# A two-layer hybrid decoder step: operand reloads by quarters, an earlier reload, and the second layer's modulation moved

## The chip, the cores and the metric

The kernel runs on one core of one Trainium2 chip. The metric is the device time of one execution in microseconds (us); the kernel before has a median of 2805.24 us over 3 runs (2802.8 to 2806.19). One further execution was taken by the profiler; all rows below come from it.

## The reference

One inference step of a two-layer trunk on 1024 prompt tokens and 8 sample tokens, in float32. Every layer has a token mixer and an MLP; both get a normalised input that is scaled and shifted by a modulation computed from a condition `c`, and both are gated by it:

```
for l in range(DEPTH):                              # 2 layers, D_MODEL = 1024
    mod = silu(c) @ ada_w[l] + ada_b[l]             # 6 * 1024 columns a layer
    sh1, s1, g1, sh2, s2, g2 = split(mod, 6)
    h = rmsnorm(x, norm_mix[l]) * (1 + s1) + sh1
    out = even_mixer(h) if l == 0 else mamba_mixer(h)
    x = x + g1 * out
    h = rmsnorm(x, norm_mlp[l]) * (1 + s2) + sh2
    x = x + g2 * (square(relu(h @ mlp_w1[l])) @ mlp_w2[l])
y = rmsnorm(x, norm_final)
```

The even mixer is a gated linear recurrence beside a short gated convolution, with one input and one output projection; the odd one is a state-space mixer. The recurrent states are returned too.

## The kernel before, in words

**Stages.** The program is one stream of work in four stages, each with its own pools of tiles: the even mixer, the first MLP, the odd mixer, the second MLP. Activations are kept transposed, features on the 128 partitions and the 1032 tokens along a row. Every float32 product of a GEMM is made of three matmuls: weights and activations are each split into a rounded part and a remainder (`hi`, `lo`), and `mm3` (L486) issues hi*hi, hi*lo and lo*hi into one PSUM sum (its three matmuls are L490, L493 and L494). ScalarE (ACT) makes `hi` by a copy, VectorE (DVE) `lo` by a subtraction: L466/L467 and others in `prep` for weights, L843/L844 for the MLP's second operand.

**Work order.** `work_order` lists every weight unit (128 x 1024) in the order of its use. `need` (L478) hands out the next one and calls `prepare`, which keeps the units ahead loaded and split: loads go from SP's queue (`dma`, L221), with two buffers for raw weights and three for split ones. `need` also calls `ada_steps(ada_rate[0])`, so that the modulation's generator makes one step a unit. `Background.tick` (L147) advances other generators (norms, recurrences) between tiles. Other transfers go from POOL's queue through `dma_aux` (L227). Some instructions are pinned to program order (`keep_in_program_order`); otherwise the framework places them in its queues, and each queue runs in order.

**Modulation.** `ada_gen` (L288) works for groups of four blocks of 512 modulation columns. A step loads four tiles of 256 KB (`t<-ada`), `depth` steps ahead, and adds one 128-row slice of the four blocks at once in PSUM (L320). After a group's eight steps a tail copies the sum, transposes it (L332) and adds the bias (L344). One layer's weights are 25 MB. In the even stage the rest of layer 0's modulation (blocks 6 to 11) runs during the last projections, one step a `need` (L1327), in tiles taken by turns from two pools (`t2` with 8, `t3` with 14 buffers). All of layer 1's runs in the first MLP's second half, one step a unit from unit 8 on (L942, L1927), in tiles from `t2` and `t6` (4 double buffers, which the weights of some products use as well).

**The MLP** is written as two levels of seven block products (a Strassen-like scheme) instead of eight. Its first half makes 16 pairs of hidden blocks, seven products each (`AOPS`). The last four pairs (12 to 15) make their products 1 and 2 first (`FRONT`): results are spilled to DRAM (`keep`, `B`) and come back later (`kept`, L854, `t<-kept`; the B12 block, `x<-b`). Product 6 of pair 12 subtracts from the reloaded tile at L899; it is the next one after `FRONT`. The seven operands of the second half are stored to DRAM while the hidden blocks are made (`td<-x`).

The second half (L938 on) does seven products of eight units each (`BOPS`, product index `i` from 0, unit `j` in 0 to 7), the last one in two halves by tokens. A unit takes a quarter `q` of the operand: units 0 to 3 use quarters 0 to 3 for the first two output blocks, 4 to 7 use them again for the other two; product 0 has its own order. `load_op` (L833) brings one half of an operand (two quarters) back in four DMAs of 516 KB into two tiles, one for `hi`, one for `lo`; three pairs of such tiles are used in rotation (`BSET`), so a half is asked for when the half three before it is done: after unit 5 of the product before, or after unit 7 of the one before that (L977). `split_op` issues the splits of loaded parts, so many after each unit as the tables at L974 to L976 say. In products 2 and 3 of this count each unit of weights is a sum of two loaded blocks and is also stored (`sd<-t`).

Of the kernel before, what the change touches and what calls it, by code (L numbers as in the profile page):

```python
# [14 lines left out]
P = 128  # L15
D = 1024
KT = 8
# [114 lines left out]
class Background:  # L132


    def __init__(self):
        self.gens = []
        self.width, self.rate, self.due = 2, 1.0, 0.0

# [23 lines left out]
def kernel(ctx: ExitStack, tc: tile.TileContext, A: dict):  # L162
# [188 lines left out]

    ada, ada_rate = [iter(())], [1]

# [431 lines left out]
    def mlp(l, gi, finish, more=None):  # L785
# [47 lines left out]
        def load_op(i, kh):  # L833

            pool, tag = ((big, M["tags"][0]), (ph.pool, "hr"), (big, M["tags"][1]))[BSET[i][kh]]
            ts = [pool.tile([P, KT * 520], F32R, name="rr", tag=tag, bufs=2) for _ in range(2)]
            hi, lo = R[i, kh] = [t[:, 0:KT * HX].rearrange("p (k t) -> p k t", t=HX) for t in ts]
            d = td[BOPND[BPROD[i]]][kh]

            def parts():  # L840
                for c in range(0, KT, 2):
# [4 lines left out]
            for c in range(0, KT, 2):  # L846
# [18 lines left out]
        for i, (p, q) in enumerate(AOPS):  # L865
# [55 lines left out]
            if (p, q) == FRONT[1][-1]:  # L921
                load_op(0, 0)
            elif p == NPAIR - 2 and q in (7, 5, 4, 3):
                split_op()
            if (p, q) == (NPAIR - 1, 5):
                split_op(4)
                load_op(0, 1)
# [5 lines left out]
        load_op(1, 0)  # L933
        acc = tp.tile([P, KT, NS], F32, name="racc", tag="racc", bufs=2)
# [4 lines left out]
        for n, (i, hb, q, mp) in enumerate(BOPS):  # L939
            j = n % 8  # L940
            hi, lo = need(f"b{l}", n, AHEAD - 1)
            if n == 8 and more:  # L942
# [3 lines left out]
            rh, rl = R[i, q // 2]  # L946
            seq = BSEQ if i else BFIRST
            qs = [qq for qq, mm in seq if mm == mp]
            for m in (2 * mp, 2 * mp + 1):
# [3 lines left out]
                for b in range(2) if hb is None else (hb,):  # L953
                    c = slice(b * hw, b * hw + hw)
                    mm3(pt[:, b, 0:hw], [(hi[:, o:o + P], lo[:, o:o + P], rh[:, k, c], rl[:, k, c])
                                         for k, o in ((q % 2 * 4 + k, 256 * k + m % 2 * P) for k in range(4))],
# [1171 lines left out]
```

## Time and profile before

| What | Value |
|---|---|
| median of 3 runs | 2805.24 us |
| the profiled execution | 2806.7 us |
| its span, first to last instruction | 2804.9 us |
| PE busy in 300 to 500 us (even layer's end) | 200 of 200 us |
| longest idle of PE in the first MLP's first half's last pairs | 5.29 us at 835.37 |
| the same in the second MLP | 6.56 us at 2396.69 |
| first MLP's second half, product 0 to 5 | 883.5 to 1223.3 us |
| second MLP's second half, product 0 to 5 | 2444.2 to 2736.1 us |
| HBM read and written | 408.59 MB, 113.80 MB |

Rows of waits read: who waited <- for whom: us in total, times, longest. Rows of the timeline: start, length, engine, line, operation, tiles written <- read, count, and in brackets the idle time before and what ended it. An instruction's row names a line of the kernel; `L490` to `L494` are the three matmuls of all GEMMs. The granted clock is the share of full speed that TensorE's throttle allowed.

### The profile page before, as it was taken

The page shows a single profiled execution, that of the slowest core. Times are in us where ns is not written, and L with a number is a line of the kernel's source. Part 1 is how long each engine was busy: PE and PEld are TensorE (multiplying, and loading weights), DVE is VectorE, ACT ScalarE, POOL GpSimd, SP SyncE. Part 2 cuts the span into 40 slices and gives each one's busy share as a digit, 9 for nine tenths or more (in the row PEclk, how much of TensorE's full clock was granted, in tenths as well). Part 3 has the DMA queues.
Part 4 walks back from the last instruction along what each step waited for, and adds up shares of the span by engine and source line. Part 5 has one row for each costly group of instructions (what it writes and reads, how often), then busy time and mean ns, then how long its engine had stood idle before and what let it go on. Part 6 is the DMA issues. An engine that isn't in the chain of part 4 may idle for free. (4 is left out here: it accounts for less than half of the span.)

```text
span 2804.9 us, 49250 instructions
## 1 busy us (share of the span) xinstructions
PE 2654.7 (95%) x19442; PEld 2443.9 (87%) x19442; DVE 1983.5 (71%) x3668; ACT 1485.0 (53%) x2409; POOL 266.5 (10%) x492
## 2 busy tenths in 40 slices
PE   6999999999999988998899999999999999999897
PEld 4889888899999977898789897787779999999897
DVE  5666544788757555775789788998778776756676
ACT  5785511464444322356687767878756445433234
POOL 0000000023223100000000000000001322311000
PEclk9999999999999999999899999999999999999998
DMA  8232333257468899834545745444435655779764
GB/s 300 69 107 71 105 121 113 88 191 242 168 204 312 328 334 353 321 129 115 142 148 144 184 122 155 132 132 124 117 105 172 223 184 181 264 284 372 266 214 156
DMA packets 199256, 525.63 MB, mean 187 GB/s; under 512 B 32688, under 2 KB 50736, under 8 KB 199024
## 3 DMA queue, kind: packets, MB, share of 16 engines
q1 hardware_dynamic: 150640, 355.25, 40.3%
q0 software_dynamic: 48384, 167.23, 16.2%
q8 instruction: 153, 2.51, 0.4%
q14 instruction: 79, 0.65, 0.1%
HBM read 408.59 MB, written 113.80 MB: 186 GB/s over the span
## 5 line engine op out<-in xcount | busy, mean ns | idle before, releaser
L490 PE MATMUL pg<-hh,whi 128*128 128x256 f32 (+2 forms) x1616 | 535.8, 332 | 13.5 <-ACT hh L592 6.2
L493 PE MATMUL pd<-rr,whi 128*128 128x258 f32 x1792 | 512.3, 286 | 25.1 <-DVE rr L844 24.9
L493 PE MATMUL pg<-hl,whi 128*128 128x256 f32 (+2 forms) x1616 | 522.8, 324 | 1.9 <-DVE hl L593 1.9
L494 PE MATMUL pg<-hh,wlo 128*128 128x256 f32 (+2 forms) x1616 | 522.0, 323 | 0.0
L490 PE MATMUL pd<-rr,whi 128*128 128x258 f32 x1792 | 513.4, 287 | 0.0
L494 PE MATMUL pd<-rr,wlo 128*128 128x258 f32 x1792 | 510.5, 285 | 1.5 <-DVE wlo L467 1.1
L467 DVE TENSOR_TENSOR wlo<-raw,whi 128x1024 fp32r<-128x1024 f32 x222 | 270.7, 1221 | 216.5 <-ACT whi L466 209.9
L466 ACT CAST whi<-raw 128x1024 fp32r<-128x1024 f32 x222 | 231.4, 1044 | 349.4 <-PE pg L493 192.0
L493 PEld LDWEIGHTS pd<-rr,whi 128*128 128x128 f32 x1792 | 343.6, 192 | 29.2 <-DVE rr L844 27.0
L490 PEld LDWEIGHTS pd<-rr,whi 128*128 128x128 f32 x1792 | 343.7, 192 | 19.0 <-issue 16.5
L490 PEld LDWEIGHTS pg<-hh,whi 128*128 128x128 f32 x1616 | 308.0, 191 | 50.0 <-issue 8.8
L494 PEld LDWEIGHTS pd<-rr,wlo 128*128 128x128 f32 x1792 | 344.0, 192 | 4.0 <-DVE wlo L467 1.8
L493 PEld LDWEIGHTS pg<-hl,whi 128*128 128x128 f32 x1616 | 308.1, 191 | 31.1 <-issue 5.8
L494 PEld LDWEIGHTS pg<-hh,wlo 128*128 128x128 f32 x1616 | 307.4, 190 | 24.4 <-issue 0.7
L490 PE MATMUL pd<-hh,whi 128*128 128x258 f32 x1024 | 293.9, 287 | 18.6 <-DVE t L899 12.6
L493 PE MATMUL pd<-hh,whi 128*128 128x258 f32 x1024 | 292.7, 286 | 0.8 <-DVE hh L695 0.8
L494 PE MATMUL pd<-hh,wlo 128*128 128x258 f32 x1024 | 291.1, 284 | 0.0
L490 PEld LDWEIGHTS pd<-hh,whi 128*128 128x128 f32 x1024 | 196.8, 192 | 21.0 <-issue 13.6
L456 ACT CAST whi<-t 128x1024 fp32r<-128x1024 f32 x64 | 67.0, 1047 | 274.8 <-PE pd L493 116.8
L493 PEld LDWEIGHTS pd<-hh,whi 128*128 128x128 f32 x1024 | 196.3, 192 | 1.9 <-DVE hh L695 1.4
L494 PEld LDWEIGHTS pd<-hh,wlo 128*128 128x128 f32 x1024 | 196.6, 192 | 0.0
L490 PE MATMUL pg<-ffh,whi 128*128 128x264 f32 (+2 forms) x544 | 176.8, 325 | 2.1 <-ACT bcz L1633 1.5
(335 smaller groups left out, 5813.9 us busy)
## 6 DMA issues: line engine op xcount, KB each, us to landing
raw<-W SPq DMA_DIRECT2D x375, 512.0 KB, 4.3
td<-x POOLq DMA_DIRECT2D x224, 258.0 KB, 3.6
rr<-td POOLq DMA_DIRECT2D x112, 516.0 KB, 8.1
t<-ada SPq DMA_DIRECT2D x192, 256.0 KB, 5.4
t<-W SPq DMA_DIRECT2D x32, 512.0 KB, 5.8
sd<-t SPq DMA_DIRECT2D x32, 512.0 KB, 5.8
t<-sd SPq DMA_DIRECT2D x32, 512.0 KB, 5.5
t<-csd SPq DMA_DIRECT2D x64, 256.0 KB, 4.6
```

The source lines that it names most:

```text
L456: S.copy(hi, h)
L466: S.copy(hi, raw)
L467: V.tensor_sub(lo, raw, hi.bitcast(F32))
L490: mm = PE.matmul(pt, wh, xh, start=first and i == 0, stop=False)
L493: PE.matmul(pt, wh, xl, start=False, stop=False)
L494: PE.matmul(pt, wl, xh, start=False, stop=last and i == n - 1)
```

## The change

It does three things.

- **Operand loads by quarters.** `load_op(i, q)` loads one quarter, `hi` and `lo` side by side in one tile, in two DMAs of the same 516 KB. A tile is free when its quarter's last unit is done. From product 1 on, quarters 2 and 3 of the next product are asked for after units 4 and 5, quarters 0 and 1 of the one after that after units 6 and 7 (product 0: after 2, 3, 6, 7). The split tables follow.
- **One reload earlier.** The tiles that pairs 12 and 13 need from DRAM, and pair 12's B12 block, are asked for at product 1 of pair 15, two products earlier than before, and so ahead of the four loads of the second half's first operand instead of behind them.
- **Two thirds of layer 1's modulation** (blocks 0 to 7, 16 steps and two tails) run in the even layer's end after layer 0's rest, loaded two steps ahead. Steps there are no longer tied to `need`: `mm3` counts its columns, and `Background.tick` makes a step whenever 8200 more have gone by. Blocks 8 to 11 (8 steps, one tail) stay in the first MLP's second half, one step in four units from unit 4 on. `ada_rate` is 0 from there on.

```diff
     def tick(self, n=1):
 
+        if self.between:
+            self.between()
...
+    cols, ada_cols = [0, 0], 8200
+
+    def ada_between():
+        while cols[0] >= cols[1]:
+            cols[1] += ada_cols
+            ada_steps(1)
...
     def mm3(pt, trip, first=True, last=True):
         n = len(trip)
+        cols[0] += 3 * n * trip[0][2].shape[-1]
...
-        def load_op(i, kh):
-
-            pool, tag = ((big, M["tags"][0]), (ph.pool, "hr"), (big, M["tags"][1]))[BSET[i][kh]]
-            ts = [pool.tile([P, KT * 520], F32R, name="rr", tag=tag, bufs=2) for _ in range(2)]
-            hi, lo = R[i, kh] = [t[:, 0:KT * HX].rearrange("p (k t) -> p k t", t=HX) for t in ts]
-            d = td[BOPND[BPROD[i]]][kh]
+        def load_op(i, q):
+
+            pool, tag = ((big, M["tags"][0]), (ph.pool, "hr"), (big, M["tags"][1]))[BSET[i][q // 2]]
+            t = pool.tile([P, KT * 520], F32R, name="rr", tag=tag, bufs=2)
+            hi, lo = R[i, q] = [t[:, j * 4 * HX:(j + 1) * 4 * HX].rearrange("p (k t) -> p k t", t=HX)
+                                for j in range(2)]
+            d = td[BOPND[BPROD[i]]][q // 2][:, q % 2 * 4:q % 2 * 4 + 4]
...
-            if p in SPLIT and q == (5 if p < 2 else 6):
+            if p in SPLIT and q == (5 if p < 2 else 6) and p != NPAIR - TAIL:
                 dma_aux(slot(p, 1), B[p])
+            elif (p, q) == (NPAIR - 1, 1):
+                kept(NPAIR - TAIL)
+                kept(NPAIR - TAIL + 1)
+                dma_aux(slot(NPAIR - TAIL, 1), B[NPAIR - TAIL])
...
-            if n == 8 and more:
+            if n == 0 and more:
                 ada[0] = more()
             elif i == 6 and hb == 0 and j == 0:
                 ada_steps(99)
+            elif n % 4 == 0:
+                ada_steps(1)
...
-            if i == 0:
-                split_op((0, 2, 2, 0, 1, 1, 2, 0)[j])
-            else:
-                split_op((2, 2, 1, 1, 1, 1, 0, 1)[j] if i == 1 else (2, 1, 1, 1, 1, 1, 0, 1)[j] if i < 6 else (2, 1, 0, 0, 0, 0, 0, 0)[j] if hb == 0 else 0)
-            if j == (5 if i else 3) and i < 6:
-                load_op(i + 1, 1)
-            elif j == 7 and i < 5:
-                load_op(i + 2, 0)
+            split_op(((0, 2, 1, 1, 1, 1, 1, 1), (2, 2, 1, 1, 1, 1, 0, 2), (1, 1, 0, 0, 0, 0, 0, 0))[2 if i == 6 else i][j]
+                     if i in (0, 1, 6) else (1, 1, 1, 1, 1, 1, 0, 2)[j])
+            at = (4, 5, 6, 7) if i else (2, 3, 6, 7)
+            if j in at and i < 6 and i + 1 + at.index(j) // 2 < 7:
+                load_op(i + 1 + at.index(j) // 2, (2, 3, 0, 1)[at.index(j)])
...
-        ada[0] = ada_gen(0, alloc, ((6, 7, 8, 9), (10, 11)))
+
+        def gens():
+            yield from ada_gen(0, alloc, ((6, 7, 8, 9), (10, 11)), 2)
+            yield from ada_gen(1, alloc, ((0, 1, 2, 3), (4, 5, 6, 7)), 2)
+        ada[0], ada_rate[0] = gens(), 0
+        cols[1], bg.between = cols[0], ada_between
...
         bg.width = 1
+        bg.between = None
...
-        mlp(0, mi(0, 5), to_odd, more=lambda: ada_gen(1, alloc, ((0, 1, 2, 3), (4, 5, 6, 7), (8, 9, 10, 11))))
+        mlp(0, mi(0, 5), to_odd, more=lambda: ada_gen(1, alloc, ((8, 9, 10, 11),)))
```

More of the change, by code (lines that the diff above doesn't have):

```diff
@@ L845, in parts @@
                     yield
-            for c in range(0, KT, 2):
+            for c in range(0, 4, 2):
                 dma_aux(lo[:, c:c + 2].bitcast(F32), d[:, c:c + 2])
@@ L926, in mlp @@
                 split_op(4)
-                load_op(0, 1)
+                load_op(0, 2)
+                load_op(0, 3)
             bg.tick(2)
@@ L955, in mlp @@
                     mm3(pt[:, b, 0:hw], [(hi[:, o:o + P], lo[:, o:o + P], rh[:, k, c], rl[:, k, c])
-                                         for k, o in ((q % 2 * 4 + k, 256 * k + m % 2 * P) for k in range(4))],
+                                         for k, o in ((k, 256 * k + m % 2 * P) for k in range(4))],
                         q == qs[0], q == qs[-1])
```

7 lines of the change are left out of this document (5 added, 2 removed).

## The prediction

> **What bounds the kernel now.** I read the page's head first, then TensorE (PE) in windows cut at the products' first matmuls, then who PE waited for in the windows that fall short, then the queues behind those waits.
>
> ```profile
> span 2804.9 us, 49250 instructions
> ...
> PE 2654.7 (95%) x19442; PEld 2443.9 (87%) x19442; DVE 1983.5 (71%) x3668; ACT 1485.0 (53%) x2409; POOL 266.5 (10%) x492
> ```
>
> PE is busy for 95% of the span, so the change can only pay where PE stands still or runs at half clock, and whatever it adds to a full PE costs its whole length. The windows below give PE, PEld, DVE, ACT and POOL (us busy, instructions), then the granted clock, the DMA share and GB/s.
>
> ```profile
> 650.00:700.00 50.00, 50.00 (x420) 50.00 (x419) 41.05 (x69) 21.35 (x36) 16.51 (x31) 1.00 0.70 237
> 810.00:850.00 40.00, 34.71 (x272) 34.54 (x271) 21.24 (x35) 15.03 (x27) 11.27 (x21) 0.91 0.63 211
> 2370.00:2410.00 40.00, 33.44 (x267) 33.26 (x267) 20.89 (x35) 14.67 (x26) 11.29 (x21) 0.91 0.60 207
> 1000.50:1010.80 10.30, 5.49 (x25) 5.49 (x26) 8.62 (x10) 2.00 (x2) 0.00 (x0) 0.50 0.94 350
> 883.50:929.50 46.00, 46.00 (x387) 46.00 (x386) 22.50 (x26) 18.91 (x21) 14.35 (x27) 1.00 1.01 388
> 929.50:983.70 54.20, 54.20 (x443) 47.37 (x441) 31.99 (x42) 17.03 (x18) 4.98 (x10) 1.00 0.86 303
> 983.70:1119.20 135.50, 116.72 (x885) 101.64 (x882) 72.68 (x99) 31.07 (x33) 7.57 (x15) 0.91 0.95 342
> 1119.20:1170.30 51.10, 51.10 (x422) 47.21 (x421) 38.27 (x47) 18.85 (x20) 4.18 (x8) 1.00 0.91 335
> 1170.30:1223.30 53.00, 47.97 (x386) 47.76 (x385) 32.06 (x39) 19.00 (x21) 4.19 (x8) 0.94 0.51 190
> 2490.20:2536.20 46.00, 46.00 (x387) 46.00 (x386) 29.90 (x40) 16.06 (x16) 4.19 (x8) 1.00 0.61 210
> 2536.20:2640.00 103.80, 94.37 (x770) 93.75 (x770) 71.84 (x92) 32.08 (x32) 8.37 (x16) 0.97 0.89 332
> 2640.00:2689.50 49.50, 46.48 (x386) 46.07 (x386) 36.99 (x46) 16.99 (x18) 4.19 (x8) 1.00 0.74 257
> 2689.50:2736.10 46.60, 46.34 (x386) 46.03 (x385) 31.99 (x39) 18.90 (x21) 4.19 (x8) 1.00 0.54 193
> 362.90:511.80 148.90, 148.90 (x957) 124.72 (x960) 66.28 (x134) 24.96 (x39) 0.00 (x0) 1.00 0.32 102
> ```
>
> The first row is the MLP's full rate: 420 matmuls in 50 us, 8.4 a us, 0.119 us each. A product of the MLP's second half is 8 units of 48 matmuls: 46.0 us, as 883.5 to 929.5 shows (product 0 of the first MLP; 1 to 5 follow, the windows 983.7 and 2536.2 holding products 2 and 3). The first MLP's products 1 to 5 take 54.2 + 135.5 + 51.1 + 53.0 = 293.8 us against 5 x 46.0 = 230.0; the second MLP's, without modulation, 46.0 + 103.8 + 49.5 + 46.6 = 245.9. The waits of PE in 800 to 850, 950 to 1250 and 2500 to 2750, and one matmul of the second MLP's first half, say why.
>
> ```profile
> PE pd L490 <- DVE t L899: 5.3, 1, 5.3
> ...
> PE pd L493 <- DVE rr L844: 12.4, 2, 7.4
> PE pd L320 <- DMA t<-ada: 11.2, 3, 4.9
> ...
> PE pd L493 <- DVE rr L844: 12.4, 5, 7.1
> ...
> 2396.69 0.55 PE L490 MATMUL pd<-hh,whi 128*128 128x258 f32 x1 [6.56 <-DVE t L899]
> ```
>
> Three places, then: a reloaded tile late for L899 (both MLPs), split operands late (both), modulation weights late (first MLP). Each is a transfer.
>
> **The change part by part.** *The early reload.* POOL's queue around the first stall:
>
> ```profile
> 816.61 0.54 POOL L227 DMA_DIRECT2D kept<-t  x1 [0.70 <-ACT t L893]
> 823.01 0.54 POOL L227 DMA_DIRECT2D b<-t  x1 [5.86 <-ACT t L804]
> 823.54 2.12 POOL L227 DMA_DIRECT2D rr<-td  x4
> 825.65 1.08 POOL L227 DMA_DIRECT2D t<-kept  x2
> ```
>
> The reload (t<-kept) that L899 needs is issued behind four operand loads of 516 KB. The change issues it two products (5.7 us) before those, near 816.6, where POOL is idle. The stall was 5.3 us with the reload at 825.65, so 9 us earlier leaves nothing to wait for; late next is only the weight preparation, whose windows before show no wait. Nothing waits behind the moved issues but the stores at 816.61 and 823.01, by at most 1.6 us, and their readers come much later. Saved: at 8.4 a us the windows 810 and 2370 should hold 336 and hold 272 and 267, so 64 and 69 are missing, 7.6 + 8.2 = 15.8 us. I leave 0.8 as residue: **-15.0** (bounds -16 and -11, should DVE's queue give 5 back).
>
> *Operand loads by quarters.* Today half an operand, 2.1 MB, is asked for at once, twice within 11.5 us:
>
> ```profile
> 2573.32 2.09 POOL L227 DMA_DIRECT2D rr<-td  x4 [34.73 <-PE pd L494]
> 2584.81 2.09 POOL L227 DMA_DIRECT2D rr<-td  x4 [9.40 <-PE pd L494]
> ```
>
> In products 2 and 3 each unit also moves 1.57 MB of weights and stored sums. From the first burst to the first use of that half, four units (23 us), 4.2 + 6.3 = 10.5 MB are wanted: 456 GB/s, over the 388 that the fullest window shows. Weights land late, DVE blocks on them, and the split behind them in its queue (L844) is late. With quarters of 1.06 MB after units 4, 5, 6 and 7, the same 4.2 MB share six units (34.5 us) with 9.4 MB: 395 GB/s, about what the queues carry, and the needed quarter is split one unit earlier. Products 4 and 5 store nothing and want less. The number of DMAs and of L843/L844 instructions stays the same. New is that a split issued one unit after its load can hold ACT and DVE; behind it stand the weight preparations, due two units (11.5 us) later, which covers one landing of the median here:
>
> ```profile
> rr<-td POOLq DMA_DIRECT2D x112, 516.0 KB, 8.1
> t<-ada SPq DMA_DIRECT2D x192, 256.0 KB, 5.4
> ```
>
> The second MLP loses 245.9 - 230.0 = 15.9 us today; I expect 3 to stay: **-12.9** (bounds -16 and 0).
>
> *Two thirds of the modulation moved.* The groups of L320 in the even layer's window and in the first MLP's second half, and three waits of the queues (SP's in the two stretches, DVE's in the second):
>
> ```profile
> L320 PE MATMUL psm<-t,ct x88: 592/592/617, 362.9 to 511.4; 128*32 128x512 f32 x88
> ...
> L320 PE MATMUL pd<-t,ct x192: 592/617/1061, 941.1 to 1141.4; 128*32 128x512 f32 x192
> ...
> SPq L221 <- PE psm L320: 50.0, 5, 21.0
> ...
> SPq L221 <- DMA sd<-t: 52.7, 14, 9.8
> ...
> DVE t L455 <- DMA raw<-W: 26.4, 7, 8.6
> ```
>
> 192 matmuls are 24 steps of 8. Product 1 took 54.2 - 46.0 = 8.2 us more with 7 of them: 1.17 us each. So of the first MLP's 293.8 - 230.0 = 63.8 us, 24 x 1.17 = 28.1 are modulation, about 1.4 (an estimate from the same row: ten matmuls' worth) its three transposing tails, and 34.3 are stalls. 16 steps and two tails move: 16 x 1.17 + 0.9 = 19.6 us leave here and arrive in the even layer, where the window 362.9 to 511.8 has PE busy for all of its 148.9 us. That is **0**: no idle time there to fill.
>
> What moves for profit is 16 x 1.05 = 16.8 MB of reads, from windows with a DMA share of 0.86 to 0.95 to one with 0.32 and 102 GB/s. What stays in the first MLP is one step in four units. Products 2 and 3 then want the second MLP's 332 x 103.8 = 34.5 MB and four steps, 38.7 MB. PE needs 92.0 + 4 x 1.17 = 96.7 us for them. At 342 GB/s that is 113 us, at 388 100 us, and at 332/0.89 = 373 104 us: 3 to 16 us too long, less what three prepared units (about 4 MB, 10 us) carry over. I take 6 there, nearest to 373, and 3 for the other products, where product 0 is full already (share 1.01) and gets one step more; one of four double tiles is held by a waiting step throughout, which the 52.7 us that SP waited for stores to free such tiles warns of. Of 34.3 us 9 stay: **-25.3** (bounds -34 and -11). The Trainium skill's page "HBM Reference", section "Specifications (TRN2)", puts a core streaming alone at about 425 GB/s; by that figure the 38.7 MB take 91 us, PE is the bound and the sum comes out 6 us lower. The trace disagrees while it is full: 342 at a share of 0.95.
>
> In the even layer a step is due every 8200 columns: 8200/258 x 0.119 = 3.8 us of matmuls and 1.1 of its own, 4.9 us. The tiles are loaded two steps ahead: 8.7 us, against four issues and a landing of 5.4, some 7 us. Where two steps fall on one tick (a 512-token block is 12,288 columns) the lead shrinks. SP's queue is in order, and the tiles come from two pools. A walk through the ticks with a landing of 4.5 us gives 2 us of waits, with 6 us 8. I take **+3** (bounds 0 and +10).
>
> *Sum.* -15.0 - 12.9 + 0 - 25.3 + 3 = -50.2. The profiled execution took 2806.7 us (span 2804.9): 2756.5. It stood 1.5 above the median of the runs, 2805.24, so against that: **2755**.
>
> How much a stall costs beyond its idle time matters here. The idle times are 5.3 + 6.6, 23.6 and 12.4, 47.9 us, and I count 15.8 + 34.3 + 15.9 = 66.0, since PE comes back at half clock: in the row 1000.5 to 1010.8 the clock is 0.50 throughout, over 5.5 us of restarted work. The Trainium skill, "TensorE: Matmul & The Clock Gate", Part 1, says that work is slow for about one window of 3.4 us after an idle window; by that rule six stalls over 3.4 us add 1.7 each, 58.1 in all, and the change would end 8 us later, near 2763. The 5.5 us of this trace stand against it.
>
> **The rivals.** *Transfers stay the bound.* The bytes are the same but for the moved reads, and their shape in time matters little. Then products 2 and 3 of the first MLP take 113 us, 16 too many, its product 5 keeps its 7 us (53.0 against 46.0), so 23 of 34.3 stay; the second MLP keeps its 15.9. Gain 11.3 + 15.0 - 3 = 23.3: 2782. For it speaks the share of 1.01 in product 0; against it the 0.61 in the second MLP's product 1, idle just before the bursts. The Trainium skill, "DMA: Bandwidth & Descriptors", section "Issuing engines are not separate DMA queues", would side with it, as transfers of all queues share 16 engines; no product's window here beats 388, however many queues run.
>
> *Modulation starves the even layer.* If pools or SP's order leave only one step in flight, a load asked for at one step meets the next 3.8 us later, needs 7, and PE waits 3.2 us in each of 28 steps: 90 us, which makes 2755 - 3 + 90 = 2842, slower. It decides from a lead of one step on; at half the steps it would cost 45 and end near 2797. For it speak the 50.0 us that SP waited for L320 to free tiles, up to 21.0 at once, with one step in flight; against it 8 and 14 tiles in the two pools, of which the convolutions hold some 8, leaving three steps' worth.
>
> *The change does little of what it says.* Where pins are off, instructions are placed by the framework, and reload and quarters could end up behind the same loads; with no gain in transfers either: 2800 to 2810.
>
> **How the numbers follow.** The forecast has 0.75, its own range 2738 (every stall gone) to 2770. Transfers stay the bound 0.16, starving 0.05 (0.02 of it near 2797, faster by little), no effect 0.04. The range reaches to the second case: 2738 to 2786. A measurement can tell 0.2%, 5.6 us. Faster: 0.75 + 0.16 + 0.02 = 0.93; same 0.04; slower 0.03.
>
> **What would show it.** No wait for L899 at the start of either MLP's last pairs; loads of 1.06 MB in twos (rr x2) one unit apart; products 1 to 5 of the first MLP near 249 us and of the second near 233; PE waiting under 5 us for L320 in the even layer, whose stretch to the last output projection is some 19 us longer, with its DMA rate about doubled. Wrong it is if PE waits on t<-ada there step after step, or if products 2 and 3 stay above 106 us in both MLPs.

## The result, and the profile after

The changed kernel takes 2779.16 us (median of 4 runs, 2773.81 to 2782.21) against 2805.72 for the kernel before beside it (2802.8 to 2807.12): a ratio of 0.9905, 95% interval 0.9887 to 0.9922. It is faster by 26.6 us, a little under 1%. The forecast was 2755, a gain of 50 us, so about half of it came. The range of 2738 to 2786 held the result only because it had been drawn to reach the rival "Transfers stay the bound" with its 2782, and the result lies beside that rival.

The profiled execution, the longest of the four, took 2782.21 us. The page's head and engines:

```profile
span 2780.4 us, 49337 instructions
...
PE 2650.3 (95%) x19442; PEld 2440.7 (88%) x19442; DVE 1983.1 (71%) x3668; ACT 1485.1 (53%) x2409; POOL 266.2 (10%) x492
```

The same matmuls in a span 24.5 us shorter. The windows are cut as they were before: the even layer's end, then products 0, 1, 2 with 3, 4 and 5 of the first MLP, then 1, 2 with 3, 4 and 5 of the second. Columns: PE, PEld, DVE, ACT and POOL (us busy, instructions), granted clock, DMA share, GB/s.

```profile
362.90:535.70 172.80, 172.80 (x1111) 130.45 (x1110) 67.17 (x140) 25.62 (x40) 0.00 (x0) 1.00 0.56 189
901.50:948.70 47.20, 47.20 (x395) 46.22 (x393) 24.32 (x29) 17.35 (x19) 15.49 (x30) 1.00 1.02 401
948.70:997.10 48.40, 48.40 (x404) 46.48 (x400) 33.72 (x49) 17.92 (x18) 4.14 (x9) 1.00 0.75 265
997.10:1099.00 101.90, 97.46 (x804) 93.17 (x800) 70.54 (x89) 31.97 (x33) 8.40 (x17) 1.00 0.97 362
1099.00:1152.80 53.80, 49.48 (x400) 48.28 (x397) 33.55 (x39) 16.75 (x19) 3.59 (x7) 0.97 0.75 262
1152.80:1206.20 53.40, 48.81 (x387) 48.63 (x386) 33.87 (x43) 18.89 (x21) 3.15 (x6) 0.94 0.48 157
2461.70:2507.70 46.00, 46.00 (x385) 46.00 (x385) 30.09 (x38) 17.00 (x17) 4.19 (x8) 1.00 0.60 207
2507.70:2608.00 100.30, 95.11 (x771) 94.50 (x770) 69.98 (x91) 32.06 (x32) 8.39 (x16) 0.97 0.91 337
2608.00:2666.50 58.50, 49.87 (x386) 49.25 (x385) 40.71 (x52) 17.19 (x18) 4.19 (x8) 0.94 0.69 233
2666.50:2712.60 46.10, 46.10 (x387) 46.10 (x386) 30.11 (x36) 18.89 (x21) 3.15 (x6) 1.00 0.52 176
```

Read the lengths first. The first MLP's products 1 to 5 went from 293.8 to 48.4 + 101.9 + 53.8 + 53.4 = 257.5 us, where 249 was expected. The second MLP's went from 245.9 to 250.9, where 233 was expected: products 2 and 3 gained 3.5 us, product 4 lost 9.0. Now the DMA share beside the length: product 4 of the second MLP is the longest of all and moves only 233 GB/s on average.

Whole stages, from the first matmul of each to that of the next (us, before and after), add up to the 24.5 within rounding:

| Stage | before | after | difference |
|---|---|---|---|
| up to the first MLP | 541.0 | 564.9 | +23.9 |
| first MLP, first half | 342.5 | 336.6 | -5.9 |
| first MLP, products 0 to 5 | 339.8 | 304.7 | -35.1 |
| first MLP, product 6 | 50.9 | 52.1 | +1.2 |
| odd layer, not touched | 834.3 | 827.8 | -6.5 |
| second MLP, first half | 335.7 | 329.5 | -6.2 |
| second MLP, products 0 to 5 | 291.9 | 297.0 | +5.1 |
| second MLP, product 6 | 57.3 | 56.2 | -1.1 |

The odd layer's 6.5 us belong to no part of the change: in the profiles of the twelve runs below it takes between 829.7 and 840.8 us.

TensorE's waits in the windows 940 to 1260 and 2500 to 2720 (who waited <- for whom: us, times, longest; in the kernel before, L856 was L844, L467 was L457, L477 was L467 and L992 was L971):

```profile
PE pd L504 <- DVE rr L856: 7.6, 2, 4.3
PE pd L501 <- DVE racc L992: 5.8, 2, 4.6
PE pd L505 <- DVE wlo L477: 2.3, 1, 2.3
...
PE pd L504 <- DVE rr L856: 9.2, 4, 4.6
PE pd L505 <- DVE wlo L467: 4.6, 2, 4.2
```

The waits for modulation weights are gone, and so is the one for the reloaded tile at the start of the last pairs. What is left is all of one kind: PE waits for DVE. So the question for the experiments was what DVE waits for. In products 1 to 5 of the second MLP three waits of PE are over 4 us: one for the subtraction of a weights unit (L467, 4.23 us, until 2618.98) and two for the split of an operand (L856, 4.65 us until 2570.88 and 4.04 until 2636.94). I followed the first of these kinds. DVE's timeline in product 4 of the second MLP (start, us, line, tiles, in brackets the idle time before), then SP's, then PE's:

```profile
2606.32 1.23 DVE L465 TENSOR_TENSOR t<-t,raw 128x1024 f32<-128x1024 f32 x1 [6.43 <-DMA t<-W]
2607.46 1.22 DVE L467 TENSOR_TENSOR wlo<-t,whi 128x1024 fp32r<-128x1024 f32 x1
2608.59 1.23 DVE L856 TENSOR_TENSOR rr<-rr 128x1032 fp32r<-128x1032 f32 x1
2616.56 1.22 DVE L465 TENSOR_TENSOR t<-t,raw 128x1024 f32<-128x1024 f32 x1 [6.74 <-DMA t<-W]
2617.71 1.22 DVE L467 TENSOR_TENSOR wlo<-t,whi 128x1024 fp32r<-128x1024 f32 x1
```

```profile
2597.45 0.33 SPq L224 DMA_DIRECT2D t<-W  x1
2599.91 7.98 SPq L224 DMA_DIRECT2D raw<-W  x2
2608.70 0.33 SPq L224 DMA_DIRECT2D t<-W  x1
```

```profile
2614.47 0.28 PE L504 MATMUL pd<-rr,whi 128*128 128x258 f32 x1
2618.98 0.39 PE L505 MATMUL pd<-rr,wlo 128*128 128x258 f32 x1 [4.23 <-DVE wlo L467]
```

A weights unit of products 2 to 5 is the sum or the difference of `t` and `raw` (L461 to L465, called the addition below), and both are loaded. The subtraction at 2607.46 (L467) is done with its `t` tile at 2608.68; SP asks for the next `t` at 2608.70, into the tile that came free; it is there 7.9 us later, and the addition at 2616.56 starts. Behind it in DVE's queue stands the next subtraction, 2617.71, for which PE has waited 4.23 us. So a unit took 10.25 us (2606.32 to 2616.56), where PE needs 5.75. The program's own queue orders name the tiles. DVE's, beside SP's, in the changed kernel:

```
DVE  L465 t6_27905 <- t6_27905 + raw_27907       SP  t6_27905 <- W     (waits for DVE)
DVE  L467 wlo_27702 <- t6_27704                  SP  raw_27966 <- W    (waits for DVE)
DVE  L856 rr                                     SP  raw_28025 <- W    (waits for DVE)
DVE  L465 t6_27964 <- t6_27964 + raw_27966       SP  t6_27964 <- W     (waits for DVE)
DVE  L467 wlo_27765 <- t6_27767
```

The DVE rows are those from 2606.32 to 2617.71. There are four `t` tiles (27704, 27767, 27839 and 27905 hold them here), so 27964 gets the tile of 27704, which the subtraction at 2607.46 frees. Its addition stands in DVE's queue ahead of the subtraction of 27767, the next one that PE needs. Each step waits for the one ahead: subtraction, load, addition, subtraction.

The two waits for an operand's split have additions ahead of them in DVE's queue too, which had waited 4.27 us (the one at 2564.39) and 2.09 us (at 2633.38). But in the second case ACT finished the copy that the split needs only at 2634.0, behind a copy of weights for which it had waited 3.79 us for PE, and the split began at 2635.66. So DVE's order accounts for less than half of that wait of 4.04 us.

The average of 233 GB/s over product 4 does not mean that the transfer engines had room while these loads were under way. The same columns as in the windows above, in steps of 4 us:

```profile
2596.00:2600.00 4.00, 4.00 (x36) 4.00 (x35) 3.79 (x4) 2.01 (x2) 1.05 (x2) 1.00 0.87 286
2600.00:2604.00 4.00, 4.00 (x35) 4.00 (x35) 0.00 (x0) 1.05 (x1) 1.05 (x2) 1.00 0.99 354
2604.00:2608.00 4.00, 4.00 (x36) 4.00 (x35) 1.69 (x2) 0.00 (x0) 0.00 (x0) 1.00 0.93 370
2608.00:2612.00 4.00, 3.64 (x31) 3.43 (x30) 1.82 (x2) 2.96 (x3) 1.05 (x2) 1.00 0.84 256
2612.00:2616.00 4.00, 2.75 (x23) 2.54 (x22) 0.00 (x0) 1.57 (x2) 0.00 (x0) 1.00 0.71 270
2616.00:2620.00 4.00, 1.02 (x8) 1.02 (x9) 3.44 (x5) 0.43 (x1) 0.00 (x0) 1.00 0.34 99
```

The `t` load of 2597.45, used at 2606.32, fell into steps with a share of 0.87 to 0.99; the one of 2608.70 into 0.84 and 0.71. The share is low (0.34) when PE already stands still. So at least the first of the two loads was late while the engines were nearly full, which the average over the product hides.

### The profile page after: what moved, and what is told of

Same layout as the page of the kernel before. It is cut to its first block, busy times and chain, and to the rows that moved or that the text cites. A ratio compares the mean times of both kernels' runs of the same rounds, so it can differ in the third digit from the quotient of the medians.

```text
span 2780.4 us, 49337 instructions
## 1 busy us (share of the span) xinstructions
PE 2650.3 (95%) x19442; PEld 2440.7 (88%) x19442; DVE 1983.1 (71%) x3668; ACT 1485.1 (53%) x2409; POOL 266.2 (10%) x492
## 5 line engine op out<-in xcount | busy, mean ns | idle before, releaser
L477 DVE TENSOR_TENSOR wlo<-raw,whi 128x1024 fp32r<-128x1024 f32 x222 | 271.1, 1223 | 219.8 <-ACT whi L476 212.7
L501 PEld LDWEIGHTS pg<-hh,whi 128*128 128x128 f32 x1616 | 308.1, 191 | 55.8 <-issue 15.8
```

What stands on the lines that cost most here:

```text
L477: V.tensor_sub(lo, raw, hi.bitcast(F32))
L501: mm = PE.matmul(pt, wh, xh, start=first and i == 0, stop=False)
```

## The experiments

The runs below were made in four groups, each on one chip beside the kernel before, which took 2815.67 to 2823.01 us there (medians of the groups). The first four rows of the table are one group; the rows "no stores", "two and two" and "the changed kernel again" another; the last row one by itself; the rest the fourth. So ratios are compared, with their 95% intervals. Products 1 to 5 are the sums of their lengths in the profile, in us; 5 x 46.0 = 230.0 is the floor, and about 8.7 of modulation come on top in the first MLP where two thirds of it have been moved. A length comes from one profile and moves by some us without a cause in the edit: the changed kernel has 250.9 and 248.7 us in the second MLP in its two profiles, and "reload alone" and "modulation alone", which leave the source of that stretch as it was, have 252 where the profile before has 245.9.

| Kernel | ratio | interval | first MLP, 1 to 5 | second MLP, 1 to 5 |
|---|---|---|---|---|
| reload alone | 0.9946 | 0.9928 to 0.9965 | 294.8 | 251.9 |
| quarters alone | 0.9993 | 0.9975 to 1.0012 | 293.8 | 249.5 |
| modulation alone | 0.9966 | 0.9951 to 0.9981 | 257.2 | 252.4 |
| all but quarters | 0.9907 | 0.9878 to 0.9936 | 259.3 | 254.4 |
| the changed kernel again | 0.9903 | 0.9889 to 0.9918 | 258.1 | 248.7 |
| its additions behind the split | 0.9866 | 0.9843 to 0.9890 | 251.3 | 245.1 |
| its additions in program order | 0.9865 | 0.9846 to 0.9884 | 256.9 | 239.3 |
| all but quarters, additions behind the split | 0.9847 | 0.9827 to 0.9867 | 253.6 | 242.3 |
| no operand loads | 0.9753 | 0.9731 to 0.9776 | 239.3 | 231.2 |
| no stores of weight sums | 0.9884 | 0.9867 to 0.9902 | 255.7 | 249.1 |
| operand loads two and two | 0.9864 | 0.9850 to 0.9879 | 248.5 | 243.3 |
| halves, new order, more raw tiles | 0.9839 | 0.9810 to 0.9867 | 257.9 | 242.7 |

### The three parts, one by one

**The reload alone**, on the kernel before:

```diff
-            if p in SPLIT and q == (5 if p < 2 else 6):
+            if p in SPLIT and q == (5 if p < 2 else 6) and p != NPAIR - TAIL:
                 dma_aux(slot(p, 1), B[p])
+            elif (p, q) == (NPAIR - 1, 1):
+                kept(NPAIR - TAIL)
+                kept(NPAIR - TAIL + 1)
+                dma_aux(slot(NPAIR - TAIL, 1), B[NPAIR - TAIL])
```

> The kernel before with the early reload alone (loads by halves, modulation where it was). Both theories: the waits at the subtraction after FRONT go in both MLPs, first halves near 336.5 and 329.5 us instead of 342.5 and 335.7, time near 2793 (2791 to 2796). If the order of the queues elsewhere shifts with it, the second halves move by more than 2 us and the time leaves that range.

0.9946, or 15.2 us of 2817 (9.9 to 20.3 by the interval). POOL's queue shows the move (`t<-kept` ahead of the four `rr<-td`):

```profile
821.55 1.07 POOL L227 DMA_DIRECT2D t<-kept  x2
822.61 0.54 POOL L227 DMA_DIRECT2D x<-b  x1
...
828.84 2.11 POOL L227 DMA_DIRECT2D rr<-td  x4
```

**The quarters alone**, on the kernel before:

```diff
-            if j == (5 if i else 3) and i < 6:
-                load_op(i + 1, 1)
-            elif j == 7 and i < 5:
-                load_op(i + 2, 0)
+            at = (4, 5, 6, 7) if i else (2, 3, 6, 7)
+            if j in at and i < 6 and i + 1 + at.index(j) // 2 < 7:
+                load_op(i + 1 + at.index(j) // 2, (2, 3, 0, 1)[at.index(j)])
```

with `load_op` and the split tables as in the change.

> The kernel before with operand loads by quarters alone. Theory of the forecast (bursts of 2.1 MB make the weights late, spreading them removes it): the second MLP's products 1 to 5 fall from 245.9 us to about 233, the first MLP's also fall, time 2780 to 2793. Rival (each unit's weights are one loop of load, addition, release, and any operand load beside it makes that loop slower than PE, so that spreading only spreads the delay): products 1 to 5 of the second MLP stay at 245 to 253 us and the time is 2803 to 2812.

0.9993: nothing. The stalls only moved. In the second MLP products 2 to 5 took 47.1, 52.1, 58.1 and 46.1 us; with halves, in the run with the reload alone, 47.9, 55.8, 49.6 and 52.6. The sum of 249.5 us lies where the rival of this expectation had it, 245 to 253.

**The modulation alone**, on the kernel before:

```diff
-            if n == 8 and more:
+            if n == 0 and more:
                 ada[0] = more()
...
+            elif n % 4 == 0:
+                ada_steps(1)
```

with the column counter in `mm3`, `ada_between`, the tick and the even layer's generators as in the change.

> The kernel before with the modulation moved alone (operand loads by halves, late reload). Theory of the forecast: the first MLP's products 0 to 5 fall from 339.8 us to about 302 (19.6 moved work and about half of 34 us of stalls, bursts staying), the even layer gets 20 to 24 us longer, time 2788 to 2795. Rival (the weights' loop): the same stalls go with the modulation whatever the operand loads do, products 0 to 5 near 300 or below, time 2783 to 2790.

0.9966, 9.6 us: under half of its share. The products of the first MLP gave 35.5 us (339.8 to 304.3 for 0 to 5, nearer to the forecast's 302 than to the rival's 300 or below), and the first MLP began 27.3 us later than in the profile of before (with the steps moved it begins between 564.3 and 571.1 us in all profiles, without between 541.0 and 548.0).

**All but the quarters**, with the quarter hunks of `load_op` and the split tables taken out of the changed kernel (the last diff in reverse).

> The changed kernel without the quarters: early reload and modulation moved, operand loads by halves as before. Theory of the forecast: slower than the changed kernel by 10 us or more (2790 to 2800). Rival: no slower than it, 2770 to 2779, with the second MLP's products 1 to 5 back at 246 us from the 251 of the changed kernel.

0.9907, the same as the changed kernel. The second MLP did not go back to 246 us, as the rival of this run had it: it has 254.4. So the reload is worth what was forecast, the modulation about half, the quarters nothing, and the three add up.

### Which wait is it: the order on DVE, the bytes, or the landing?

From the timeline above comes a theory, "order": an addition that waits for a load blocks DVE's queue ahead of the subtraction that PE needs. Its rivals keep to the prediction's reason: the transfers themselves are too slow, by their bytes ("transfers", "bytes"), by their coming in bursts ("burst") or by the late landing of the operand ("lead"). "Window" came last: too few tiles to load into.

**The additions behind the split.** One thing is changed in the changed kernel: the addition for a unit is queued behind the subtraction of the unit before it.

```diff
-                if pr == 5:
-                    V.tensor_add(h, h, raw)
+                with tc.issue_after(split_b[l].ins) if l in split_b else ExitStack():
+                    if pr == 5:
+                        V.tensor_add(h, h, raw)
...
-                V.tensor_sub(lo, h, hi.bitcast(F32))
+                split_b[l] = V.tensor_sub(lo, h, hi.bitcast(F32))
```

> The changed kernel, with one thing different: the addition of two loads that makes a weights unit of products 2 to 5 is queued on DVE only behind the low-half subtraction of the unit before it, not ahead of it. The same loads, bytes and instructions. Theory 'order' (an addition whose load lands late stands at the head of DVE's queue, and the subtraction that TensorE waits for stands behind it): products 1 to 5 fall from 257.5 to about 240 us in the first MLP and from 250.9 to about 232 in the second; 25 to 38 us less than the changed kernel, a ratio to the kernel before of 0.977 to 0.982. Theory 'transfers' (the loads land when they can, and TensorE waits for them whatever stands first on DVE): the five products stay within 3 us of 257.5 and 250.9, ratio 0.989 to 0.992.

0.9866 against 0.9903, and products 1 to 5 shorter by 6.8 and 3.6 us: a gain, but some third of what theory "order" promised. The two intervals just touch; those of the three next runs with a new order (0.9865, 0.9847 and, further down, 0.9864) lie clear of the changed kernel's. Product 5 of the first MLP fell from 54.6 to 46.1, product 4 of the second from 57.3 to 52.3; product 3 did not gain. What SP waits for changed with it. In products 2 and 3 of the second MLP, first in the changed kernel (2507.7 to 2608), then in this one (2509.7 to 2610.4):

```profile
SPq L224 <- DVE t L465: 37.1, 11, 6.3
SPq L224 <- DVE wlo L467: 25.2, 12, 6.3
SPq L224 <- DVE t L461: 12.5, 5, 4.5
SPq L224 <- DMA raw<-W: 4.2, 2, 3.3
SPq L224 <- DMA sd<-t: 1.5, 2, 0.8
```

```profile
SPq L224 <- DMA sd<-t: 78.9, 15, 8.7
SPq L224 <- DVE wlo L468: 2.3, 4, 1.3
...
```

SP waited for DVE for 74.8 us; now it waits for DVE for 5.9 in all, and for the store of a sum (`sd<-t`) for 78.9. A sum is stored from its `t` tile, and the tile is free only when the store has landed. The same four tiles, with another holder.

**The additions in program order**, behind the evacuations too (`tc.keep_in_program_order(V.tensor_add(h, h, raw))` and the same for the two others).

> The changed kernel, with the same additions kept in program order on DVE: behind everything written before them, the evacuations of TensorE's sums at the fourth and eighth step of a product too. Theory 'order': nearly the gain of the other order (ratio 0.977 to 0.984), less whatever the additions lose where they now stand behind an evacuation and the unit is needed 11.5 us later (evacuation about 7, addition, copy and subtraction 3.5). Theory 'transfers': ratio 0.989 to 0.994.

0.9865, the same. SP waits for the store here as well (73.1 us in products 2 and 3 of the second MLP, 2516.1 to 2615.1).

**All but the quarters, with the additions behind the split** (the diff of the first of these runs, on the kernel of 0.9907).

> Early reload and moved modulation without the quarters (the kernel of 0.9907), and the addition behind the previous unit's low-half subtraction. Theory 'order': once no addition blocks DVE, a load of a half or of quarters is the same: products 1 to 5 at 240 to 245 and 230 to 237 us, ratio 0.977 to 0.984. Theory 'transfers', in which quarters only spread what must be carried: 259 and 254 us as without the new order, ratio 0.989 to 0.992. If this one gains clearly less than the changed kernel with the same order, the quarters do have a worth that DVE's order hid.

0.9847, and 0.9866 with quarters: the intervals overlap, so the quarters have no worth that DVE's order hid.

**No operand loads.** The operands of products 2 to 6 aren't reloaded; GpSimd fills the tiles instead, and their splits stay.

```diff
-                dma_aux(lo[:, c:c + 2].bitcast(F32), d[:, c:c + 2])
+                if i < 2:
+                    dma_aux(lo[:, c:c + 2].bitcast(F32), d[:, c:c + 2])
+                else:
+                    tc.keep_in_program_order(nc.gpsimd.memset(lo[:, c:c + 2].bitcast(F32), 0.5))
```

> The changed kernel without the reloads of the operands of products 2 to 6 of the second half (loads of 1032 columns by POOL's queue): GpSimd fills those tiles with a constant, so the values are not the reference's. DVE's order is that of the changed kernel. Both theories lay the late landings to these loads; so the weights loads should land in about 4 us each, products 1 to 5 take 240 to 245 and 230 to 235 us, ratio 0.975 to 0.982. If the products stay above 250, the late landings are not from the operands' loads, and both theories are wrong in that.

0.9753, with DVE's order as in the changed kernel. Nearly all of the stalls are gone: 239.3 and 231.2 us. Products 2 to 5 of the second MLP:

```profile
2499.30:2545.40 46.10, 46.10 (x387) 46.10 (x386) 35.94 (x44) 16.04 (x16) 7.45 (x8) 1.00 0.84 288
2545.40:2591.40 46.00, 46.00 (x385) 46.00 (x385) 34.53 (x44) 16.03 (x16) 7.43 (x8) 1.00 0.70 232
2591.40:2638.30 46.90, 46.37 (x386) 46.17 (x385) 37.52 (x51) 17.93 (x19) 7.45 (x8) 1.00 0.61 193
2638.30:2684.40 46.10, 46.10 (x387) 46.10 (x386) 29.31 (x34) 18.37 (x20) 5.60 (x6) 1.00 0.28 91
```

A weights load there lands in 4.5 us (median in products 2 to 4; the trace has the landing of 11 of the 25). One row of the DMA issues:

```profile
raw<-W SPq DMA_DIRECT2D x25, 512.0 KB, 4.5
```

The longest of the 11 took 7.2 us. In the changed kernel the two `t` loads of the timeline above took 8.9 and 7.9 us to be used, but these are the late ones; in the kernel before, where the trace has 17 landings of `raw<-W` in products 2 to 4, the median is 5.8 us and the longest 11.2. The Trainium skill, "DMA: Bandwidth & Descriptors", section "Issuing engines are not separate DMA queues", says that the engines which issue share the same 16 transfer engines. The trace agrees so far that loads of SP's queue land earlier without those of POOL's.

So without the operand's loads, which go by POOL's queue, the stalls do not come. That does not yet tell how these loads cause them: the run takes 14 MB away (32.99 MB in products 2 to 4 of the second MLP against 47.44), and it also takes away the wait for the operand itself. And it speaks against reading SP's waits as the cause. In products 2 and 3 of the second MLP, where PE is not held up, SP waits for DVE as long as in the changed kernel, 70.7 us against 74.8:

```profile
SPq L224 <- DVE t L465: 31.3, 12, 5.3
SPq L224 <- DVE wlo L467: 29.3, 14, 6.2
SPq L224 <- DVE t L461: 10.1, 3, 5.4
```

A queue that loads ahead into few tiles waits for the next one to come free even when nothing is late.

**No stores of the weight sums.** DVE's order as in the changed kernel; the 16 stores of products 2 and 3 are left out in each MLP, and a weights block is read where a sum was read back.

```diff
-            while sums and sums[0][0] <= idx - 2:
-                _, d, h = sums.pop(0)
-                dma(d, h)
```

> The changed kernel, DVE's order as it is there, without the writes of the weight sums to DRAM: 16 writes of 512 KB are left out in each MLP's products 2 and 3, and where a sum was read back, a weights unit of the same size is read instead, so the values are not the reference's. A product at 46.0 us then moves about 13 MB in place of 17. Theory 'bytes' (product 3 has some 17 MB to move, 370 GB/s for all of 46 us, which the queues just reach, and a burst behind which they fall back isn't caught up): products 3 and 4 fall from 53.4 and 53.8 us to about 49 and 48 in the first MLP and from 53.6 and 58.5 to 46 to 48 in the second, ratio 0.978 to 0.983. Theory 'lead' (the operand's quarters are issued only when the step four before has freed their tile, and land too late whatever else runs): products 3 and 4 stay within 3 us, ratio 0.989 to 0.992. Theory 'order' alone: the same as 'lead', because the additions stand where they stood.

0.9884, against 0.9903 with overlapping intervals; the second MLP has 249.1 us against 248.7. In products 2 to 4 of the second MLP it moved 39.35 MB where the changed kernel moved 47.44, at 239 to 268 GB/s, and took 156.9 us against 158.8:

```profile
2519.60:2569.00 49.40, 46.88 (x387) 46.27 (x386) 34.57 (x48) 16.03 (x16) 4.20 (x8) 1.00 0.75 268
2569.00:2621.00 52.00, 47.92 (x386) 47.51 (x385) 36.31 (x45) 16.03 (x16) 4.20 (x8) 0.97 0.73 247
2621.00:2676.50 55.50, 49.63 (x387) 48.81 (x385) 39.45 (x50) 17.07 (x18) 4.20 (x8) 0.94 0.72 239
```

That is against theory "bytes", which promised 46 to 48 us for products 3 and 4. In the first MLP product 3 did fall, from 53.3 us to 48.7, where that theory had 49, but product 4 rose from 53.2 to 56.6, where it had 48: the stall moved on. Fewer bytes over the whole stretch are not enough, then. Whether the engines are full while the operand's quarters come isn't settled by that: the `t` load that came latest in the second MLP (asked for at 2616.63, landed 8.6 us later, used in product 4) fell into a stretch with a DMA share of 0.97, at 340 GB/s. With the stores gone and the old order kept, SP waits for DVE again (in products 2 and 3):

```profile
SPq L224 <- DVE t L462: 40.0, 12, 6.9
SPq L224 <- DVE wlo L464: 35.0, 16, 6.6
```

**The operand's loads two and two.** With the additions behind the split, and in the second MLP products 1 to 5 in the step order of product 0, so that tiles come free after units 2, 3, 6 and 7.

```diff
-            seq = BSEQ if i else BFIRST
+            seq = BFIRST if i == 0 or l and i < 6 else BSEQ
...
-            at = (4, 5, 6, 7) if i else (2, 3, 6, 7)
+            at = (2, 3, 6, 7) if i == 0 or l and i < 6 else (4, 5, 6, 7)
```

> The changed kernel with the additions behind the previous split, and in the second MLP the steps of products 1 to 5 in the order of product 0 (the two halves of the columns alternate after two quarters of the operand, not after four). The tiles of the operand then come free in steps 2, 3, 6 and 7 and not in 4, 5, 6 and 7: the same bytes, the loads two and two rather than four in a row, and ten steps ahead of their use rather than six. The first MLP is left as it was (modulation holds a fourth sum tile there). Theory 'burst' or 'lead' (it is the row of four loads, 456 GB/s asked for 23 us, or their late issue, that the units wait behind): products 3 and 4 of the second MLP fall from 54.6 and 52.3 us to 46 to 48 each, ratio 0.980 to 0.984. Theory 'bytes' (all of product 3 is at the limit of the queues): together still over 102 us, ratio 0.985 to 0.989.

0.9864 against 0.9866: no difference. Products 2, 3 and 4 took 50.1, 49.1 and 51.9 us where they took 46.1, 54.6 and 52.3. Spread loads spread the stalls. Theories "burst" and "lead" fall, as far as the operand's loads are concerned: they had 46 to 48 us each for products 3 and 4. Theory "bytes" had over 102 for the two together; they took 101.0, and product 2 took 4 more.

**The changed kernel again**, beside the others, without an edit.

> The changed kernel again, beside the others, for the comparison within one call: ratio 0.989 to 0.992 if the earlier one holds here.

0.9903: the first comparison's 0.9905 holds on this chip.

**Halves, the new order, more raw tiles.** Every other unit's second load goes into two half-size tiles that are idle.

```diff
-                raw = load_unit(*second)
+                if idx % 2:
+                    raws = [t2(512), t2(512)]
+                    for r, c in zip(raws, (0, 512)):
+                        dma(r, A["W"][WIDX[second]][:, c:c + 512])
```

> Early reload and moved modulation, halves in place of quarters, the additions behind the previous split (0.9847), and one thing more: every other weights unit of products 2 to 5 takes its second load not into the two raw tiles but into two free half-size tiles, so that up to four more such loads can be in flight before an addition has freed one (two loads of 256 KB and two additions of 512 columns in place of one of each). Theory 'window' (two raw tiles let only two such loads be in flight; beside the operand's loads each lands in 7 to 9 us and not in 4, so a unit every 5.75 us isn't reached): products 1 to 5 take 242 to 247 us in the first MLP (253.6 without the tiles) and 230 to 234 in the second (242.3), ratio 0.978 to 0.982. Theory 'lead' (the operand's own late landing and split decide, however early the weights are there): within 3 us of 253.6 and 242.3, ratio 0.983 to 0.987. The first MLP's modulation rows use the same half-size tiles, so the second MLP is the cleaner reading.

0.9839 against 0.9847 without these tiles, and 242.7 against 242.3 us in the second MLP: theory "window", as far as it meant the raw tiles, falls. (The first MLP got 4.3 us longer, 257.9; its modulation uses the same half-size tiles.) SP waited for the store, in products 2 and 3 of the second MLP:

```profile
SPq L224 <- DMA sd<-t: 82.0, 15, 8.9
SPq L224 <- DVE wlo L474: 0.9, 1, 0.9
```

What SP waits for here is the `t` tile; that more of these would help was not tried. Apart from the two runs that leave work out, the two kernels with halves and the new order are the fastest here: 0.9847 (0.9827 to 0.9867) against 0.9903 (0.9889 to 0.9918) for the changed kernel.

**What is shown and what is not.** Shown: the reload and the moved modulation carry the gain, the quarters add nothing; without the operand's loads nearly all stalls go; with 8 MB of stores less the sum of the stalls stays; another order on DVE takes away 10 us (0.0037 of 2816), and SP's waits pass over from DVE to the stores. Argued, not shown: that the stalls come from the loop of tile, load, addition and subtraction rather than from transfer engines that are full while the operand's quarters land. Each may have its part. The new order and no stores together, a fifth `t` tile, and another order of the copies on ACT weren't run; nor is it known how much of the landing time is due to each queue.

## Why the prediction was half right

**The early reload: right.** -15.0 forecast, 15.2 measured alone. That the two agree to 0.2 us is luck: the interval of the measurement is 9.9 to 20.3, and in the profiles the two first halves gave 5.9 + 6.2 = 12.1 us, within the bounds.

**The moved steps: right in sum.** 19.6 us of PE work and 3 of waits were to arrive in the even layer; the first MLP starts 23.9 us later, in a window where PE is busy throughout (172.80 of 172.80), and the DMA rate went from 102 to 189 GB/s. No wait of PE for these loads is there, so the 3 us of waits did not come. The moved matmuls take 18.9 us (L323 30.2 us for 12.4, L335 2.4 for 1.3); 2 us the changed kernel was behind before these steps began (the same matmul of the projections starts at 343.3 us for 341.2); the last 3 lie in a PE that is busy throughout and have no reason that I know. That 22.6 and 23.9 lie so near is in part luck. "Modulation starves the even layer" did not happen.

**The first MLP's stalls: the mechanism right, the size off.** 34.3 us were to become 9, by bytes: 38.7 MB at 373 GB/s. Products 1 to 5 have 257.5 - 230.0 - 8.7 = 18.8 us of stalls left (8.7 being seven steps of 1.17 and a tail of 0.5), so the term was -15.5, not -25.3. Products 2 and 3 came out nearly as calculated, 101.9 us at 362 GB/s. The stalls that were not foreseen are in products 4 and 5, 53.8 and 53.4 us, at 262 and 157 GB/s; "3 for the other products" had put them aside; of products 4 and 5 the prediction says that they "store nothing and want less". The figure of 425 GB/s that the prediction set beside this, from the Trainium skill's page "HBM Reference", section "Specifications (TRN2)", was not decisive: product 0 moved 401 GB/s over 47.2 us without a wait, and the products that stalled were below that on average.

**The quarters: wrong.** The step that failed is "the same 4.2 MB share six units (34.5 us) with 9.4 MB: 395 GB/s, about what the queues carry, and the needed quarter is split one unit earlier". -12.9 was forecast and nothing came, alone or with the rest. Two things in it failed. First, 395 GB/s left no room: in the second MLP, from the first quarter's load at 2537.61 to PE's wait at 2566.23, the engines moved 385 GB/s at a share of 0.99, and PE still waited 4.65 us. Second, product 4 was put at next to nothing (3 us were to stay in all five products), and there the longest stalls are: 58.5 us for 46.0. From the first quarter's load at 2591.15 to PE's wait at 2614.75 the rate was 302 GB/s at a share of 0.87, well below 395, so the rate alone does not explain it; 8 MB less in three products left the sum of the stalls as it was. What the trace shows there is the loop: subtraction, load, addition, and in the queue's order the next subtraction behind it, 10.25 us for a unit of 5.75 while a `t` load took 7.9. How much of the stalls is this order and how much the landing time stays open: the new order took away 10 us, while 18.8 and 20.9 us of stalls stand in the two MLPs. The prediction had the pieces. It wrote that "Weights land late, DVE blocks on them, and the split behind them in its queue (L844) is late", and quoted the 52.7 us that SP waited for stores to free such tiles. It took DVE's block as the effect of a rate alone, and did not ask which instruction frees the tile that the late load goes into.

**What a stall costs.** In the second MLP's products 1 to 5 PE is busy for 46.00 + 95.11 + 49.87 + 46.10 = 237.1 of 250.9 us: 13.8 of idling for 20.9 over the floor, so 7.1 of slow work after it. After the three waits over 4 us the granted clock is 0.51 over 2568.8 to 2575.7, 2620.0 to 2623.5 and 2637.1 to 2640.6, with PE busy for 4.8, 3.5 and 3.5 us of them: some 2.4, 1.7 and 1.7 us lost. Half clock for 3.4 us, as the Trainium skill's "TensorE: Matmul & The Clock Gate", Part 1, has it, would give 1.7. Two of the three waits agree with that; the first, and the 5.5 us of the trace of before (2.75 lost), are longer.

**The sum.** Forecast -50.2 against the profiled execution, measured -24.5. Missing are 2.9 of the reload, 1.3 in the even layer, 9.8 in the first MLP's products 0 to 5 (304.7 for 339.8 - 19.6 - 25.3 = 294.9) and 17.9 in the second's products 1 to 5 (250.9 for 233); the odd layer's 6.5 go the other way.

**The rivals.** "Transfers stay the bound" comes nearest with its time, 2782, but not with its reason. It had products 2 and 3 of the first MLP at 113 us; they took 101.9. Its second MLP, which "keeps its 15.9", is nearer too: 20.9 us over the floor, where I had 3. Its "their shape in time matters little" holds for the quarters, yet 8 MB alone were taken away without a gain that can be measured. The mark that I had set for being wrong, products 2 and 3 above 106 us in both MLPs, did not trip: 101.9 and 100.3. It looked at the products in which the stalls had been, and they had gone on to the next ones.

## What to carry to other kernels

When a load is late, ask what freed the tile that it went into, and what stands behind the instruction that waits for it: a ring of few tiles and an in-order queue can close a loop whose period is a landing time plus the instructions in it. Read the waits of the queue that issues the loads beside those of the engine that computes: they name the holder of the tile, and when one holder is removed the next shows there. Then read them in a run that does not stall as well: here they were as long there (70.7 us against 74.8), so they name the holder but not the cause. Cut a rate into steps as short as the load in question before calling the transfer engines idle. Where a stall sits in one of several like stages, forecast and check the sum over all of them, because a change in the shape of transfers tends to move it to the next.

## What the runs showed of the hardware

How long a 512 KB weights load takes to land depends on what else is in flight. For `raw<-W` in products 2 to 4 of the second MLP, median and longest: 4.5 and 7.2 us without the operand's loads (237 GB/s on average), 4.3 and 6.3 us with them but without the stores of sums (251 GB/s), 5.8 and 11.2 us in the kernel before, with both (307 GB/s); the trace has the landing of 11, 17 and 17 of the 25 loads. In these three runs the landing time is longest where the average rate is highest. An average over a product hides the full stretches: product 4 of the changed kernel has 233 GB/s, and 286 to 370 GB/s at a share of 0.87 to 0.99 while the load that took 8.9 us was under way.
